# Retention gate of a hybrid decoder step by seven half-size products, its place in the retention loop given to a head's key and query projection, and two smaller reorderings

## The chip, the cores and the metric

One core of one Trainium2 chip runs the whole program. The metric is the time of one execution in microseconds on the device. A kernel's time is the median of several executions; one more execution is taken with the hardware profiler, and all rows below come from that one.

## What is computed

The reference is one layer of a decoder for 1024 prompt tokens and 8 sample tokens (1032 columns in all, model width 1024). The parts that matter here:

```python
hp = rmsnorm(xp, norm_mix)
qa, ka, va, qr, kr, vr, gr = split(hp @ w_in)        # widths 512 512 512 256 256 512 512
oa  = diff_attention(qa, ka, va)                     # 4 heads, two softmax maps each
s, o_r = retention(rotary(qr), rotary(kr) * 64**-.5, vr)   # 4 heads, 8 chunks of 128 tokens
r   = head_rms(o_r) * silu(gr)                       # the retention gate
xp  = xp + concat(head_rms(oa) * subln * (1 - lam_init), r) @ w_out
...                                                  # memory cross-attention
xp  = xp + square(relu(rmsnorm(xp) @ w_up)) @ w_down # hidden width 4096
```

All weights and activations are float32. A large product is made of three matmuls: both operands are split into a rounded high part and a low part, and high x high, high x low and low x high are summed.

## The kernel before

**Value blocks.** `token_block` computes a 1024 x 512 product over the model width 1024 with seven products of half the size in each direction instead of eight (a Strassen-like scheme, products numbered 1, 2, 6, 7, 4, 5, 3). Each product is 4 token tiles x 4 slices of 128 input rows x 3 terms = 48 matmuls of 256 columns; for the 8 sample rows four of the products add 8 narrow matmuls each (`psd`). The kernel runs it twice, for the attention values (`va`, PSUM tiles `vap_*`) and for the retention values (`vr`, tiles `vrp_*`). VectorE and ScalarE combine and scale the products and split the weights of the next one. `token_operands` loads four weight units per block through SyncE's DMA queue.

**Retention loop.** For each of 8 chunks of 128 tokens: four transposes of queries and keys (`tr`), scores (`sc`, masked on VectorE into `Sm`), the state update (`st`, added on VectorE into `S`), the output (`op`), then on ScalarE the squares of the output per head (`jk`, sums `s4`), on GpSimd their power -1/2 (`r4`), on VectorE the normalised output times the gate (`gate`, line 665), and in the next step four transposes of that (`trR`), a split into `rh` and `rl` (one buffer each), and two stores to DRAM through GpSimd's queue (`OPH`, `OPL`). Between these small matmuls TensorE does the gate projection of the same chunk, `grp`: 24 matmuls of 512 columns per chunk, dealt out 9 + 12 + 3 by `SEG`. After chunk 2 the gate of the sample rows follows (`decproj`, 16 matmuls, line 286 of the helper `dproj`). `decode_step`, in steps 0 to 3, does the sample rows' retention: GpSimd multiplies (`vb`, lines 703 and 714), VectorE state updates (`sn`). In the same steps ScalarE and VectorE rewrite half of the operand tiles `UH`, `UL` (`restore`).

**Attention.** `head_proj(0)` then makes the keys and queries of attention head 0 (144 matmuls of 344 columns, tiles `qkp`, results `kraw`, `qraw`) as filler that `fill(n)` deals out n matmuls at a time: 96 after the loop, 36 more (`START`) before the first score. `load_part` splits keys into `KA` and `KB` and copies each half to the other 64 partitions by DMA from GpSimd's queue; it splits queries into `Q`. Scores (`sp`) of map 0 and map 1 read `KA[0]`, `KB[0]` and `KA[1]`, `KB[1]`. VectorE forms `e` and its minimum `mn`, ScalarE the exponential; TensorE transposes the result (`trA`). The order of TensorE's instructions is the order of the program text (`pinned`); the other engines' order comes from the scheduler that respects `behind(...)` and `issue_after(...)`: an instruction stands behind a named one.

**Down projection.** Its left weights are loaded in four groups (`raw_d`, 8 transfers of 512 KB a group, `load_left`, line 2492), its hidden activations by `right_lower` (`raw_h`, two transfers of 516 KB per product, line 2375; products 1, 2, 6, 7, 4, 5, 3 again), all on SyncE's queue, which issues in order and waits at an instruction whose buffer is not free. TensorE works on `dn` tiles (line 2412), 169 matmuls in a stretch of 20 us.

Of the kernel before, what the change touches and what calls it, by code (L numbers as in the profile page):

```python
# [19 lines left out]
P = 128  # L20
# [28 lines left out]
def decoder_step(ctx: ExitStack, tc: tile.TileContext, i: dict, o: dict):  # L49
# [115 lines left out]
    ord_ = dram.tile([4, 8, P], F32, tag="ord", name="ord_")  # L165

# [17 lines left out]
    t_front, v_front = ExitStack(), ExitStack()  # L184
# [203 lines left out]
    with pool("a") as A:  # L388
# [6 lines left out]
        def decproj(units, name, PS, out, bufs=3):  # L395

            ps = PS.tile([P, 512], F32, tag="acc", name=name, bufs=bufs)

            dproj(ps, units)
            merge_parts(ps, out, name)  # L400
            return out

# [3 lines left out]

        def tokproj_parts(units, t, name, PS):
            ps = PS.tile([P, 512], F32, tag="acc", name=name, bufs=3)
            tk = slice(t * P, t * P + P)
            for kt in KT_PAIRS:  # L410
                w = [u[:, (kt // 4) * 512 : (kt // 4) * 512 + 512] for u in units[kt % 4]]
                mm(ps, UH[:, kt, tk], w[0], kt == 0, False)
                mm(ps, UH[:, kt, tk], w[1], False, False)
                mm(ps, UL[:, kt, tk], w[0], False, kt == 7)
                yield ps
# [64 lines left out]
        def token_block(ready, nm, out_dec, fetch, between, after):  # L480
# [12 lines left out]
            def scale(t):  # L493
                if t > 3 and nm == "vr":
                    return
                y = acc[t // 2][:, t % 2, :]
                cs = slice(256, 512) if t < 4 else slice(0, 512)
                nc.scalar.activation(y[:, cs], y[:, cs], AF.Copy, scale=rstd1[:, t : t + 1])

            order = (1, 2, 6, 7, 4, 5, 3)  # L500
            for n, q in enumerate(order):
# [13 lines left out]
                for pb in range(2):  # L515
# [14 lines left out]
                    with behind("Activation", "DVE"):  # L530
                        if q == 1:
                            nc.scalar.copy(lo[:, :, b], pv)
                        elif q == 2:
                            for j in range(2):
                                nc.scalar.activation(lo[:, j, a], pv[:, j, :], AF.Copy, scale=rstd1[:, 2 * pb + j : 2 * pb + j + 1])
# [7 lines left out]
                if q in (1, 2, 4, 5):  # L543
# [6 lines left out]
                    if q == 5:  # L550
                        merge_parts(psd, out_dec, nm)
                        nc.scalar.activation(out_dec, out_dec, AF.Copy, scale=rstd1[:8, 8:9])
# [35 lines left out]
        rot_va, rot_vr = {4: 8, 5: 0, 3: 1}, {1: 2, 2: 3, 6: 4, 7: 5, 4: 6, 5: 7}  # L588

        def after_va(q, acc):  # L590
# [8 lines left out]
            if q in rot_va:  # L599
                rotate(rot_va[q])  # L600

        def after_vr(q, acc):
            if q in rot_vr:
                rotate(rot_vr[q])
            if q == 5:
                nc.scalar.dma_start(vrd, vr8[:8])
                nc.scalar.activation(silu, half[:, 0:1], AF.Silu)
            if q in (5, 3):
                for u in range(2):
                    if q == 3:  # L610
# [2158 lines left out]
```

## Time and profile before

| | us |
|---|---|
| three runs | 1473.46, 1474.56, 1474.77 |
| median | 1474.56 |
| the profiled execution, its own time | 1475.19 |
| its span in the profile | 1473.4 |
| first matmul of the value blocks, first of the retention loop | 54.3, 143.4 |
| last `op` matmul of the loop, first score | 226.7, 249.6 |
| TensorE busy | 1455.7 |

The profiled execution took 0.63 us more than the median, and 1.8 us of it lie outside the span. Times of places in the program are microseconds from the start of the span. A busy TensorE is a sum of modelled matmul spans that overlap; what a stretch of matmuls really takes is read from the chain of work that ended last, where a run of matmuls stands with its start, its length and its count.

### The profile page before, as it was taken

The numbers are of one execution on the slowest core, as the hardware profiler recorded it, in microseconds if no ns is written. First come the engines' busy times: TensorE is split into PE (matmuls) and PEld (weight loads), VectorE is DVE, ScalarE is ACT, GpSimd is POOL, SyncE is SP. The second block draws the span as 40 slices with busy tenths as digits, with TensorE's granted clock in tenths as the row PEclk, the third lists the DMA queues.
The fourth block names the chain that finished last, engine by engine and source line by source line (L and its number), as shares of the span: only waits on it lengthen the run. The fifth ranks groups of instructions, "written<-read, shape, count | busy, mean of one in ns | idle before, by whom it ended". The sixth has DMA issues, their size and how long they took to land.

```text
span 1473.4 us, 28129 instructions
## 1 busy us (share of the span) xinstructions
PE 1455.7 (99%) x11013; PEld 1401.0 (95%) x11013; DVE 1107.9 (75%) x2263; ACT 679.7 (46%) x1327; POOL 314.4 (21%) x345
## 2 busy tenths in 40 slices
PE   9999999999999999999999999999999999999998
PEld 7899779999889999999999999999999999999998
DVE  7666536888867756567868988888888878787876
ACT  7434435666552441267436533343435443343454
POOL 0035433122304511224122000000002211110380
PEclk9999999999999999999999999999999999999998
DMA  8155738215957265654762444333446764536273
GB/s 295 62 188 171 205 70 192 72 34 159 283 169 269 100 209 170 177 178 122 236 234 77 151 159 158 138 136 133 149 159 216 262 213 144 173 105 200 71 130 116
DMA packets 129833, 238.98 MB, mean 162 GB/s; under 512 B 13606, under 2 KB 80987, under 8 KB 129572
## 3 DMA queue, kind: packets, MB, share of 16 engines
q1 hardware_dynamic: 91354, 170.66, 36.0%
q0 software_dynamic: 27472, 46.93, 11.8%
q10 hardware_dynamic: 10874, 19.60, 3.5%
q8 instruction: 86, 1.41, 0.4%
q14 instruction: 47, 0.39, 0.1%
HBM read 171.13 MB, written 58.92 MB: 156 GB/s over the span
## 4 chain that ended last, share of the span: by engine, by line
PE 88%; DVE 5%; DMA 2%; ACT 2%; issue 1%; POOL 0%; ACTq 0%; SPq 0%; DVEq 0%
PE dn L2412 20%; PE Z L2244 9%; PE qkp L75 6%; PE Y L2244 6%; PE X L2244 6%; PE mq L75 6%; PE pr_m L75 6%; PE pr_o L75 5%; PE grp L75 3%; PE sp L75 2%; PE mv L75 2%; PE mk L75 1%; PE av L75 1%; PE mpv L75 1%; PE vap_z L524 1%; PE vrp_z L524 1%
## 5 line engine op out<-in xcount | busy, mean ns | idle before, releaser
L2412 PE MATMUL dn<-UH,wd 128*128 128x258 f32 (+1 forms) x1800 | 326.6, 283 | 3.0 <-DVE c L2546 3.0
L2412 PEld LDWEIGHTS dn<-UH,wd 128*128 128x128 f32 x1800 | 279.6, 190 | 3.6 <-ACT wd L2388 2.6
L2412 PE MATMUL dn<-UL,wd 128*128 128x258 f32 x900 | 254.6, 283 | 0.0
L2412 PEld LDWEIGHTS dn<-UL,wd 128*128 128x128 f32 x900 | 170.5, 189 | 0.1
L2546 DVE TENSOR_TENSOR c<-c,dn 128x258 f32<-128x258 f32 (+1 forms) x217 | 89.1, 417 | 38.5 <-PE dn L2412 35.8
L2270 ACT ACTIVATE hq<-r 128x258 f32<-128x258 f32 x128 | 53.7, 421 | 117.4 <-DVE r L2269 117.3
L2244 PE MATMUL Z<-T_h,wu 128*128 128x258 f32 x512 | 98.1, 283 | 0.0
L2244 PE MATMUL X<-UH,wu 128*128 128x258 f32 x512 | 97.5, 282 | 0.0
L2388 ACT CAST wd<-raw_d 128x512 fp32r<-128x512 f32 x96 | 58.7, 619 | 82.0 <-PE dn L2412 77.3
L2052 ACT CAST wu<-raw_up 128x512 fp32r<-128x512 f32 x96 | 59.0, 616 | 61.0 <-PE Z L2244 52.6
L2381 ACT CAST UH<-raw_h 128x1032 fp32r<-128x1032 f32 x56 | 58.7, 1055 | 55.2 <-PE dn L2412 27.9
L2244 PEld LDWEIGHTS X<-UH,wu 128*128 128x128 f32 x512 | 81.3, 188 | 0.0
L2244 PEld LDWEIGHTS Z<-T_h,wu 128*128 128x128 f32 x512 | 81.3, 189 | 0.0
L2382 DVE TENSOR_TENSOR UL<-raw_h,UH 128x1032 fp32r<-128x1032 f32 x56 | 72.9, 1301 | 9.9 <-ACT UH L2381 9.9
L2389 DVE TENSOR_TENSOR wd<-raw_d,wd 128x512 fp32r<-128x512 f32 x96 | 72.3, 759 | 10.2 <-ACT wd L2388 10.2
L2281 POOL DMA_DIRECT2D HT<-ht x32 | 17.2, 536 | 292.1 <-DVE ht L2280 291.6
L2244 PE MATMUL Z<-T_l,wu 128*128 128x258 f32 x256 | 72.3, 282 | 0.0
L2244 PE MATMUL X<-UL,wu 128*128 128x258 f32 x256 | 72.3, 282 | 0.0
L129 ACT CAST wh_u<-raw_u 128x1024 fp32r<-128x1024 f32 x43 | 44.7, 1047 | 57.6 <-PE mq L75 39.9
L2053 DVE TENSOR_TENSOR wu<-raw_up,wu 128x512 fp32r<-128x512 f32 x96 | 64.8, 689 | 3.6 <-ACT wu L2052 3.6
L2402 POOL TENSOR_TENSOR raw_d<-raw_d,raw_d 128x512 f32<-128x512 f32 x16 | 22.1, 1384 | 197.0 <-DVE raw_d L2398 145.3
L130 DVE TENSOR_TENSOR wl_u<-raw_u,wh_u 128x1024 fp32r<-128x1024 f32 x39 | 48.6, 1257 | 20.2 <-ACT wh_u L129 20.0
(616 smaller groups left out, 4707.4 us busy)
## 6 DMA issues: line engine op xcount, KB each, us to landing
raw_u<-in_wall SPq DMA_DIRECT2D x49, 512.0 KB
HT<-ht POOLq DMA_DIRECT2D x32, 516.0 KB, 3.0
raw_h<-HT SPq DMA_DIRECT2D x32, 516.0 KB
raw_up<-in_wall SPq DMA_DIRECT2D x32, 512.0 KB
raw_d<-in_wall SPq DMA_DIRECT2D x32, 512.0 KB
HQ<-hq ACTq DMA_DIRECT2D x32, 387.0 KB
raw_h<-HQ SPq DMA_DIRECT2D x24, 516.0 KB
cmk<-in_cmk SPq DMA_DIRECT2D x16, 512.0 KB
```

Of the source, the lines that this page charges most:

```text
L75: pinned(nc.tensor.matmul(out, l, r, start=start, stop=stop))
L130: (lo_engine or nc.vector).tensor_sub(wl[:, :n], raw[:, :n], wh[:, :n].bitcast(F32))
L2052: nc.scalar.copy(w[:, :512], src)
L2053: nc.vector.tensor_sub(w[:, 512:], src, w[:, :512].bitcast(F32))
L2244: pinned(nc.tensor.matmul(ps, l, r[:, k, :], start=first and k == 0 and x == 0, stop=k == 3 and x == 2, skip_group_check=True))
L2270: nc.scalar.activation(h[:, PLACE[quad], :], r, AF.Square)
L2381: nc.scalar.copy(h, rv)
L2382: nc.vector.tensor_sub(l, rv, h.bitcast(F32))
L2388: nc.scalar.copy(w[:, :512], src)
L2389: nc.vector.tensor_sub(w[:, 512:], src, w[:, :512].bitcast(F32))
L2412: pinned(nc.tensor.matmul(ps[:, part], l, r[:, k, cq], start=first and k == 0 and x == 0, stop=k == 3 and x == 2, skip_group_check=True))
L2546: nc.vector.tensor_add(y, y, ps)
```

## The change

Four things are edited.

1. The gate becomes a third `token_block` (`ga`), between `va` and `vr`, with the sigmoid-weighted function applied where a value block scales. Its result goes to a DRAM tensor `gated` and is fetched again chunk by chunk (`fetch_gate`). `grp` and the sample rows' `decproj` go. The weights of the gate are laid out in DRAM as those of a value block. The rotations of queries and keys that ran beside `vr` now run beside `ga`.
2. In the retention loop `head_proj(0)` takes the place of `grp`: 8 filler matmuls ahead of the loop, 6 and 5 per step (`RFILL`), 96 in all; 36 are left between the loop and the first score. The transposes of the next chunk move ahead (`turn_step`); `brep` and `rb` are sent in the `vr` block; the weights of head 1 are split in steps 4 and 5.
3. `load_part` of heads 1 to 3 rounds and subtracts the keys of both maps in one instruction of 128 partitions each; the halves are then placed by four DMAs of GpSimd's queue and two of SyncE's. For head 0 the four-instruction form stays, in two pieces of 344 columns. `load_values(0)` and the loads of heads 2 and 3 move by one step.
4. `load_left` of the second group stands behind the last `raw_h` load of the first.

```diff
-        rot_va, rot_vr = {4: 8, 5: 0, 3: 1}, {1: 2, 2: 3, 6: 4, 7: 5, 4: 6, 5: 7}
+        rot_va, rot_ga = {4: 8, 5: 0, 3: 1}, {1: 2, 2: 3, 6: 4, 7: 5, 4: 6, 5: 7}
...
+        def after_ga(q, acc):
+            if q in rot_ga:
+                rotate(rot_ga[q])
+            for t in {5: range(4), 3: range(4, 8)}.get(q, ()):
+                nc.scalar.dma_start(gated[t * P : t * P + P, :], acc[t // 2][:, t % 2, :])
...
-        token_block(op_va, "va", vdec[:8], rot_va, after_va, op_vr)
+        op_ga, op_vr = token_operands(U_TOK + 8, "ga"), token_operands(U_TOK + 4, "vr")
+        token_block(op_va, "va", vdec[:8], rot_va, after_va, op_ga)
+        ga8 = A.tile([P, 512], F32, tag="t1", name="ga_8", bufs=1)
+        token_block(op_ga, "ga", ga8[:8], rot_ga, after_ga, op_vr, AF.Silu)
...
-            grp = tokproj_parts(units, t, f"grp_{t}", PS)
-            for _ in range(SEG[0]):
-                next(grp)
...
+        filler = head_proj(0)
+        dec = decode_step(0)
+        next(dec)
+        gate = fetch_gate(0)
+        turned = turn_step(0)
+        fill(RFILL[0])
+        for t in range(8):
+            qb, kT = turned
...
+            if t < 7:
+                turned = turn_step(t + 1)
+            if scaled:
+                with behind("DVE"):
+                    next(scaled)
+            fill(RFILL[1])
...
+            if pend:
+                pend()
+            fill(RFILL[2])
...
         def load_part(h, cs):
...
+            if h:
+                nc.scalar.copy(KA[1][:, cs], kraw[:, cs])
+                for x in (lo, hi):
+                    nc.gpsimd.dma_start(KA[0][x, cs], KA[1][lo, cs])
+                nc.vector.tensor_sub(KB[1][:, cs], kraw[:, cs], KA[1][:, cs].bitcast(F32))
...
+                if h:
+                    K1 = (KA, KB)[m][1]
+                    nc.sync.dma_start(K1[lo, cs].bitcast(F32), K1[hi, cs].bitcast(F32))
...
-        fill(36)
+        load_stacks(0)
+        for c in range(2):
+            for _ in load_part(0, slice(c * CH, c * CH + CH)):
+                pass
+        filler = chain(filler, rest())
+        fill(28)
         to_operand(gate, P, 7, "7", ("ah", "al", 2))
-        until(0, 1, 0)
+        fill(6)
+        to_operand(lasts[0], 8, 8, "d", ("ah", "al", 2))
...
-            load_left((0, 1) if g == 0 else range(4))
+            with tc.issue_after(seen["SP"]) if g == 1 else nullcontext():
+                load_left((0, 1) if g == 0 else range(4))
...
-START = 36
+START = 2
...
-SEG = (3, 4, 0)
+RFILL = (8, 6, 5)
```

What that does to the order is seen at three places.

SyncE's queue in the down projection, before. `raw_h0_3_0` is the first half of the hidden activations of product 3 in group 0; `raw_d1_...` are left weights of group 1; `c12` and `c21` are residual rows.

```order
L2375 DMA raw_h0_5_0_14176<-HT_75 128x4x258
L2375 DMA raw_h0_5_2_14180<-HT_75 128x4x258
L2492 DMA raw_d1_0_0_14436<-in_wall 128x1024
L2492 DMA raw_d1_1_0_14438<-in_wall 128x1024
L2375 DMA raw_h0_3_0_14184<-HQ_74 128x4x258
L2492 DMA raw_d1_2_0_14440<-in_wall 128x1024
L2375 DMA raw_h0_3_2_14188<-HQ_74 128x4x258
L2361 DMA c12_13489<-X3_73 128x516 x4
```

The same place of the changed kernel:

```order
L2392 DMA raw_h0_5_0_14375<-HT_75 128x4x258
L2392 DMA raw_h0_5_2_14379<-HT_75 128x4x258
L2392 DMA raw_h0_3_0_14383<-HQ_74 128x4x258
L2392 DMA raw_h0_3_2_14387<-HQ_74 128x4x258
L2378 DMA c12_13688<-X3_73 128x516 x4
L2509 DMA raw_d1_0_0_14635<-in_wall 128x1024
L2509 DMA raw_d1_0_1_14636<-in_wall 128x1024
L2509 DMA raw_d1_1_0_14637<-in_wall 128x1024
```

Three loads of the second group no longer stand between the loads of the first group's products 5 and 3.

TensorE in chunk 7 of the retention loop, before: the scores, the state, the transposed gate of chunk 6, and the first seven of twelve gate matmuls.

```order
L75 MATMUL sc_2267<-qblk_1566,kT_2255 128x256 x2
L75 MATMUL st_2272<-vr_1210,qk_491 64x128 x4
L78 MATMUL trR_2277<-ident,gate_2214 128x128 x4
L75 MATMUL grp_2257<-wh_u_1492,UH 128x512
L75 MATMUL grp_2257<-wl_u_1493,UH 128x512
L75 MATMUL grp_2257<-wh_u_1492,UL 128x512
L75 MATMUL grp_2257<-wh_u_1600,UH 128x512
```

The same place of the changed kernel, with all that stands between `st` and the first `op` matmul:

```order
L75 MATMUL sc_2584<-qblk_2028,kT_2526 128x256 x2
L75 MATMUL st_2589<-vr_1696,qk_492 64x128 x4
L75 MATMUL qkp_0_1_2482<-UL,wh_u_1954 128x344
L75 MATMUL qkp_0_1_2482<-UH,wl_u_1955 128x344
L75 MATMUL qkp_0_1_2482<-UH,wh_u_1954 128x344
L75 MATMUL qkp_0_1_2482<-UL,wh_u_1954 128x344
L75 MATMUL qkp_0_1_2482<-UH,wl_u_1955 128x344
L75 MATMUL qkp_0_1_2482<-UH,wh_u_1954 128x344
L75 MATMUL op_2604<-vr_1696,Sm_2587 128x128
```

Twelve matmuls of 512 columns (and in the chunks before the transposes of the next chunk) give way to six of 344, and `trR` moves behind `op`.

GpSimd from the last chunk's factor `r4_7` to the first key copies of head 0, before (`rh_7` and `rl_7` are the split gate of the last chunk, `VL_0` the low part of the values):

```order
L141 TENSOR_TENSOR r4_7_2330<-s4_7_2329,half_64 128x4
L678 DMA OPL_71<-rl_d_2352 128x4x8
L1051 MEMSET ah_0_0_0_2703 128x128
L678 DMA OPH_70<-rh_7_2427 128x4x128
L678 DMA OPL_71<-rl_7_2428 128x4x128
L1051 MEMSET al_0_0_0_2704 128x128
L995 TENSOR_TENSOR VL_0_2748<-vraw_0_2572,VH_0_2747 128x512 x2
L968 DMA KA0_0_2513<-KA0_0_2513 64x688
L970 DMA KB0_0_2515<-KB0_0_2515 64x688
```

And in the changed kernel:

```order
L141 TENSOR_TENSOR r4_7_2634<-s4_7_2633,half_64 128x4
L984 DMA KA0_0_2675<-KA0_0_2675 64x344
L986 DMA KB0_0_2677<-KB0_0_2677 64x344
L984 DMA KA1_0_2676<-KA1_0_2676 64x344
L986 DMA KB1_0_2678<-KB1_0_2678 64x344
```

The key copies of head 0 now follow the last factor directly, where two stores and the values' low part stood between.

## Rows read from the trace of the kernel before

**Rows 1.** The page: busy us, share and instructions of each engine.

```profile
PE 1455.7 (99%) x11013; PEld 1401.0 (95%) x11013; DVE 1107.9 (75%) x2263; ACT 679.7 (46%) x1327; POOL 314.4 (21%) x345
```

**Rows 2.** TensorE's waits, by what ended them: us in total, times, longest.

```profile
PE dn L2412 <- DVE c L2546: 3.0, 2, 2.4
PE trA L78 <- DVE e L1034: 2.1, 2, 1.4
PE sp L75 <- DVE mn L1019: 1.8, 2, 1.0
```

**Rows 3.** The chain in the block va: start, us, what, count.

```profile
54.29 5.68 PE vap_x L524 x48
59.98 0.94 PE vap_d L547 x8
```

**Rows 4.** The chain in the retention loop and behind it.

```profile
173.12 3.71 PE grp L286 x16
...
187.10 2.10 PE grp L75 x9
...
191.40 2.80 PE grp L75 x12
...
230.90 1.13 DVE gate L665 x4
...
234.68 9.44 PE qkp L75 x60
...
244.66 2.27 DVE wl_u L130 x2
```

**Rows 5.** Windows: length, busy us (count) PE, PEld, DVE, ACT, POOL; PEclk, DMA, GB/s.

```profile
99.00:106.00 7.00, 6.83 (x58) 6.42 (x56) 5.51 (x8) 4.21 (x7) 2.61 (x3) 1.00 0.70 231
...
156.00:166.00 10.00, 10.00 (x62) 8.12 (x61) 4.76 (x13) 3.65 (x13) 4.54 (x5) 1.00 1.04 362
187.10:197.12 10.02, 10.02 (x61) 8.10 (x61) 3.52 (x10) 3.03 (x13) 5.03 (x5) 1.00 0.43 105
...
1160.00:1180.00 20.00, 20.00 (x169) 20.00 (x169) 17.90 (x29) 9.06 (x15) 1.67 (x1) 1.00 0.81 260
1180.00:1200.00 20.00, 17.62 (x134) 17.45 (x134) 13.54 (x24) 9.60 (x13) 0.00 (x0) 0.91 0.82 281
```

**Rows 6.** Issue of `raw_h0_3_0`, and the first copy of it: start, us, what.

```profile
1174.51 0.38 SPq L2375 DMA_DIRECT2D raw_h<-HQ  x1
...
1182.78 1.06 ACT L2381 CAST UH<-raw_h 128x1032 fp32r<-128x1032 f32 x1 [5.95 <-DMA raw_h<-HQ]
```

**Rows 7.** The chain in the same place.

```profile
1163.76 3.88 DMA raw_h<-HT
...
1177.60 7.84 DMA raw_h<-HQ
...
1188.26 11.80 PE dn L2412 x84
```

**Rows 8.** GpSimd in step 1 of the retention loop: start, us, what.

```profile
164.93 1.03 POOL L141 TENSOR_TENSOR r<-s,half 128x4 f32<-128x4 f32 x1 [4.35 <-DVE s L140]
...
166.53 1.91 POOL L714 TENSOR_TENSOR vb<-sn,qkd 128x1024 f32<-128x1024 f32 x1
169.05 0.80 POOL L678 DMA_DIRECT2D OPH<-rh  x1 [0.61 <-ACT rh L675]
```

**Rows 9.** Key copies (line 968) to landing; VectorE's split of one map's keys.

```profile
DMA to landing us min/median/max: 2.3/4.4/7.7
...
276.80 0.86 DVE L969 TENSOR_TENSOR KB<-kraw,KA 64x688 fp32r<-64x688 f32 x1
```

**Rows 10.** TensorE idle at the first scores of head 0, in brackets.

```profile
262.42 0.41 PE L75 MATMUL sp<-KA,Q 128*128 128x320 f32 x1 [0.85 <-DVE mn L1019]
```

**Rows 11.** Stores of the loop, 145 to 165, then 165 to 200: KB, us to landing.

```profile
OPH<-rh POOLq DMA_DIRECT2D x1, 256.0 KB, 9.3
...
OPH<-rh POOLq DMA_DIRECT2D x3, 256.0 KB, 2.9
```

More of the change, by code (lines that the diff above doesn't have):

```diff
@@ L478, in decoder_step, with token_block @@
         PS = f_ps.enter_context(pool("f_ps", space=PSUM))
-        def token_block(ready, nm, out_dec, fetch, between, after):
+        def token_block(ready, nm, out_dec, fetch, between, after, func=AF.Copy):
             acc = []
@@ L629, in decoder_step, with fill, until @@
+        def fill(n):
+            for _ in range(n):
+                next(filler, None)
+        def until(*key):
+            while key not in done:
+                next(filler)
         pin[0] = True
-        op_vr = token_operands(U_TOK + 4, "vr")
-        token_block(op_va, "va", vdec[:8], rot_va, after_va, op_vr)
+        op_ga, op_vr = token_operands(U_TOK + 8, "ga"), token_operands(U_TOK + 4, "vr")
+        token_block(op_va, "va", vdec[:8], rot_va, after_va, op_ga)
+        ga8 = A.tile([P, 512], F32, tag="t1", name="ga_8", bufs=1)
@@ L730, in decoder_step, with fetch_gate @@
             nc.vector.tensor_copy(kT, tr[:, 256:512])
-            if t == 6:
-                with behind("DVE"):
-                    next(scaled)
-            grp = tokproj_parts(units, t, f"grp_{t}", PS)
-            for _ in range(SEG[0]):
-                next(grp)
+            return qb, kT
+        def fetch_gate(t):
+            if t < 7:
+                gate = A.tile([P, 512], F32, tag="gate", name=f"gate_{t}", bufs=3)
+            else:
+                last = G.tile([P, T], F32, tag="raw", name="gate_7", bufs=3)
+                gate = last[:, :512]
+                lasts.append(last[:8, 512:1024])
+            nc.sync.dma_start(gate, gated[t * P : t * P + P, :])
+            return gate
+        S, pend, scaled, lasts = None, None, None, []
+        filler = head_proj(0)
+        pin[0] = True
+        dec = decode_step(0)
[5 more added lines that the diff above has]
+            qb, kT = turned
             sc = PS.tile([P, 512], F32, tag="sc", name=f"sc_{t}", bufs=1)
@@ L1265, in decoder_step @@
         items = [(h, pr, kg) for h in range(4) for pr in range(4) for kg in range(pr + 1)]
-        done = set()
         EARLY, LATE = slice(0, 2 * CH), slice(2 * CH, NT)
@@ L1271, in rest @@
                 yield from head_proj(h)
-        filler = head_proj(0)
         decode = decode_steps()
-        def fill(n):
-            for _ in range(n):
-                next(filler, None)
-        def until(*key):
-            while key not in done:
-                next(filler)
-        pin[0] = True
-        fill(36)
-        to_operand(gate, P, 7, "7", ("ah", "al", 2))
-        until(0, 1, 0)
-        with behind("Activation", "DVE"):
-            head_units(1)
-        load_stacks(0)
-        for _ in load_part(0, EARLY):
-            pass
-        filler = chain(filler, rest())
+        pin[0] = True
+        load_stacks(0)
+        for c in range(2):
+            for _ in load_part(0, slice(c * CH, c * CH + CH)):
+                pass
+        with behind("Activation"):
+            nc.scalar.activation(A.tile([P, 1], F32, tag="pre", name="pre"), half[:, 0:1], AF.Exp)
+        filler = chain(filler, rest())
+        fill(28)
+        to_operand(gate, P, 7, "7", ("ah", "al", 2))
+        fill(6)
+        to_operand(lasts[0], 8, 8, "d", ("ah", "al", 2))
         par = operand_steps()
```

228 lines of the change are left out of this document (104 added, 124 removed).

## The prediction

> **What bounds the kernel now.** I read the busy shares first: TensorE is busy 1455.7 us of a span of 1473.4 [rows 1]; the next engine, VectorE, is at 75%. So the time is TensorE's work plus the few places where it waits. The list of its waits says how little that is: the largest are 3.0 us for the combination `c` of the down projection, 2.1 us for `e` ahead of the transposes of attention and 1.8 us for `mn` ahead of the scores [rows 2]. An edit can therefore gain in two ways: fewer or shorter matmuls, or one of these waits. It can lose in one: by taking away filler behind which the other engines now finish unseen. The third view, the chain of waits in the retention loop, shows an unbroken row of TensorE pieces [rows 4]: every wait in this loop is covered today. The windows add how much the other engines do there [rows 5].
>
> **The change part by part.** All sums are against the profiled execution, 1475.19 us, which lies 0.63 us over the median of 1474.56.
>
> *1. Products.* Nine `grp` matmuls take 2.10 us and twelve 2.80 us, so 0.2325 us each [rows 4]. The loop has 8 x 24 = 192 of them, 44.64 us; the sample rows' 16 take 3.71 us [rows 4]. Removed: 48.35 us. Added is a block of the form of `va` and `vr`, for which `va` has the price: 48 matmuls in 5.68 us, 0.1183 us each, and 8 narrow ones in 0.94 us [rows 3]. Seven products make 7 x 48 = 336 matmuls, 39.76 us, and four groups of narrow ones 3.76 us: 43.52 us. Net **-4.8 us**. This is the surest term, as both prices are of the same operations on the same operand types. Its check is arithmetic: seven eighths of 44.64 us would be 39.06, so half-width matmuls cost 0.7 us more for the same columns.
>
> The rows put a 256-column matmul at 0.1183 us and a 512-column one at 0.2325 us, nearly the ratio of the columns [rows 3, 4]. The Trainium skill, "TensorE: Matmul & The Clock Gate", section "Back-to-back issue gap", speaks against such a halving: in a stream of weight loads and matmuls it gives about 81 ns for 128 columns and 131 ns for 512, so a matmul four times as wide costs only 1.6 times as much. Interpolated (an estimate from that page of the Trainium skill), 256 columns would cost some 98 ns, and term 1 would be 336 x 0.098 + 3.8 - 208 x 0.131 = 9.5 us lost. Both rows here contradict that, and the measurement decides.
>
> *2. Boundaries between forms of matmul.* A step of the loop has two groups of filler instead of three between the small matmuls. No row prices a boundary; nine matmuls in a row cost no more apiece than twelve [rows 4], so it is between nothing and about half a matmul, 0.1 us: 0 to -0.8 us for eight steps. I take **-0.4**.
>
> *3. The second group's left weights.* In the window 1160 to 1180 TensorE does 169 matmuls, in 1180 to 1200 only 134 [rows 5]. The missing 35 at 0.118 us are 4.1 us: 2.4 us idle [rows 2, 5], and the rest slower matmuls, since the granted clock, at 1.00 (2.4 GHz) before, is 0.91 in the mean of this window, so at the lower level for part of it [rows 5], and 84 `dn` matmuls take 11.80 us, 0.140 each [rows 7]. The cause can be read: `raw_h0_3_0` is issued at 1174.51, behind two weight loads, and its first copy starts at 1182.78, with ScalarE 5.95 us idle for it [rows 6]; the second half takes 7.84 us [rows 7]. The same kind of load shortly before takes 3.88 us [rows 7]. With the weights behind it, it should land some 3.5 to 4.4 us earlier, which covers the 2.4 us and so the clock's fall. Its own buffer does not come free earlier, so the issue time stays; what goes is the traffic beside it. **-4.1** (0 to -4.1). The price could be that group 1 is late. Its first weights are put off by the two halves of `raw_h0_3` and the residual rows alone, some 4 us, and product 3 lies between, whose 84 matmuls in the chain are 11.8 us [rows 7]; I take nothing for it, and would lose the same 4 us if that cover were gone.
>
> *4. The retention loop with less cover.* A step lasts 10.02 us [rows 5]. Without its 5.58 us of `grp` and with 11 matmuls of `head_proj` at 9.44/60 = 0.157 us [rows 4] it lasts 4.44 + 1.73 = 6.2 us. The other engines must fit in that. VectorE is busy 4.76 us in a step of the first half and 3.52 later [rows 5]; added are about 0.5 us of `kraw`/`qraw`, so 5.3: it fits, with order and latency against it. In steps 4 and 5 come weight splits of 2.27/2 = 1.14 us each [rows 4]. GpSimd in step 1 has `r` 1.03, two `vb` of 1.91, and three stores of about 0.8: 7.2 us [rows 8], over 6.2 by about one. So some steps wait a few tenths and step 1 nearly a microsecond: **+1.9** (0 to +5, the upper end being 0.6 us in each of eight steps). At zero it would be hidden by the move of `trR` behind `op`, which gives the gate's chain almost a whole step.
>
> *5. From the loop to the first score.* Today the last gate is ready at 232.03 [rows 4], 5.3 us behind the last `op`, and the first score comes at 249.6. Afterwards the five fills of the last step and 36 more, 41 x 0.157 = 6.4 us, and some 1.5 us of transposes cover this stretch: 7.9 us. The keys of head 0 need that gate chain on VectorE (5.3), a split (about 0.5 for half the columns, half of the 0.86 of [rows 9], and as much again behind it), the issue on GpSimd (0.55), and the landing, 2.3 to 7.7 us, median 4.4 [rows 9]: 8.7 us at the lowest landing, 10.7 at the median. The wait is then 0.8 to 2.8, with a slow landing about 5; I take **+1.7**, nearer the middle, as little else is on the DMA queues there. Against it stands the 0.85 us that TensorE idles at 262.42 for `mn` [rows 10]: four splits of the next head's weights at 1.14 us [rows 4], which made VectorE late, are then done in the loop: **-0.85** (0 to -0.85).
>
> *6. One more block.* The change from `va` to `vr` costs 0.17 us in its window (7.00 less 6.83 [rows 5]); one more such place, with the sigmoid's function loaded there: **+0.3** (0.17 to 1).
>
> *7. Attention.* For three heads one split on 128 partitions takes the place of two on 64 (0.86 us each [rows 9]): VectorE saves some 3 x 1.4 = 4 us with the pieces. The waits for `e` and `mn`, 3.9 us less the 0.85 above [rows 2, 10], bound the gain at 3; two copies more by DMA per key could be late, +1. I take **-1.0** (+1 to -2.6).
>
> Sum: -4.8 - 0.4 - 4.1 + 1.9 + 1.7 - 0.85 + 0.3 - 1.0 = -7.25, so 1467.9 for such a profiled execution and 1467.3 by the median; I say 1467.5. All good ends: about -12 (1462.7); all bad ones of terms 2 to 7: +7.
>
> **The rivals.** *Loop and prelude at their upper ends* (terms 4 and 5 at +4 and +4.5 instead of +1.9 and +1.7): about 1472.5. For it: the loop has no filler left to spare, and three engines are within a microsecond of its length [rows 5, 8]. Against: `jk`'s and the gate's chain now have a step to finish.
>
> *The down projection's wait stays.* If `raw_h0_3_0` is slow for other reasons than the two weight loads (the residual rows `c12` in the same queue, or the window's traffic of 260 GB/s as such [rows 5]), term 3 is 0: 1471.4. For it: a DMA share of 0.81 before the wait begins; against: 3.88 us for the same load ahead of it [rows 7].
>
> *Slower: the stores of the loop hold up `rh` and `rl`.* These have one buffer each, so the next split waits until the store has landed. `OPH` took 9.3 us in the stretch 145 to 165, where the DMA share is 1.04, and 2.9 us in the later one [rows 5, 11]. In 10 us steps this was hidden; in steps of 6.2 us it decides from a landing of about 4.5 us on (a step less the split and the issue). Three early steps at 9.3 would cost 3 x 4.8 = 14 us, in place of the loop's 1.9: 1467.5 + 12 = 1479.5. Against: the vr block's loads, which fill the queues early in the loop, are the same in number, but the gate weights' loads now lie ahead of it.
>
> *Weight loads bind the half-width matmuls.* The mean busy time of a weight load is 1401.0/11013 = 0.127 us [rows 1], over the 0.1183 of a 256-column matmul; if each new matmul were held to that, 336 + 32 of them would take 46.7 us, term 1 would shrink to -1.6, and the time be 1470.7. `va` has the same loads at 0.1183 already [rows 3], which speaks against it. The section of the Trainium skill, "TensorE: Matmul & The Clock Gate", "Back-to-back issue gap", lets both operations set the spacing; by its figures the time would be 1481.8.
>
> *The change doesn't do what it says* (as many matmuls as before, since one product is recomputed): the order of the instructions excludes it.
>
> **How the numbers follow.** Forecast, 1464.5 to 1470.5: 0.63. Upper ends in loop and prelude, 1470.5 to 1474: 0.14. The wait in the down projection stays, 1471.4: 0.12. Slower by the stores, 1478 to 1485: 0.08. Weight loads, 1470.7: 0.02. Better than 1464.5: 0.01. About 0.2%, 2.95 us, is what a measurement of this kernel can tell from no change, so faster ends at 1471.6 and slower begins at 1477.5. Faster gets the forecast, half of the second case, half of the third and the small ones: 0.63 + 0.07 + 0.06 + 0.03 = 0.79; slower the stores: 0.08; same the rest: 0.13. The range runs from 1463, all good ends, to 1474.
>
> **What would show it.** Right: `ga` as seven products of 5.7 us in the chain; loop steps of 6.2 to 6.7 us, with VectorE or GpSimd in the chain for tenths; a wait of 1 to 3 us for the key copies before the first score; 1180 to 1200 with about 169 matmuls and a granted clock of 1.00. Wrong: steps of 8 us and more, with `rh` or `rl` idle for `OPH` or `OPL`; `ga` matmuls at more than 0.12 us; ScalarE still 4 us idle for `raw_h` at product 3, or `dn` waiting at the start of group 1; a first score more than 14 us behind the last `op`.

## The result: 0.2% slower, where 0.5% faster was forecast

| | before | changed |
|---|---|---|
| median, us (20 runs each) | 1473.66 | 1476.71 |
| lowest and highest | 1472.09, 1475.72 | 1473.67, 1480.42 |
| the profiled execution, us | 1475.19 | 1476.23 |
| ratio | | 1.0022, 95% interval 1.0016 to 1.0029 |

The changed kernel loses about 3 us; 7 less had been forecast, and the range ended at 1474.0. The page of the changed kernel answers [rows 1]: TensorE is as full as it was, with 160 more matmuls in 1.3 us less busy time.

```profile
PE 1454.4 (99%) x11173; PEld 1408.3 (96%) x11173; DVE 1118.1 (76%) x2278; ACT 680.4 (46%) x1335; POOL 318.1 (22%) x349
```

Its waits answer [rows 2]. The one in the down projection is nearly gone, as forecast, though not through the edit, as will be seen; those of attention have grown, by count above all. The wait for `mn` of [rows 10], which term 5 of the prediction counted as won, is still there: 0.91 us at 258.69.

```profile
PE trA L78 <- DVE e L1053: 3.6, 5, 1.3
PE sp L75 <- DVE mn L1038: 2.4, 4, 1.0
PE dn L2429 <- DVE c L2564: 1.2, 3, 0.6
...
PE ct L75 <- ACT sq L1096: 0.8, 1, 0.8
```

```profile
258.69 0.42 PE L75 MATMUL sp<-KA,Q 128*128 128x320 f32 x1 [0.91 <-DVE mn L1038]
```

The chain in the new block and in one step of the loop (start, us, what, count) answers [rows 3, 4]. The gate's products cost what `va`'s did, 43.6 us from 99.43 to 143.06, and a step of the loop takes 6.28 us, from 199.92 to 206.21 here; nothing but TensorE stands in it.

```profile
99.43 5.68 PE gap_x L507 x48
105.11 0.94 PE gap_d L530 x8
...
137.36 5.71 PE gap_y L507 x48
```

```profile
199.92 0.86 PE sc L75 x4
200.79 0.59 PE st L75 x8
201.38 0.59 PE tr L78 x4
201.96 0.95 PE qkp L75 x6
...
202.93 2.05 PE op L75 x16
204.99 0.44 PE trR L78 x4
205.42 0.79 PE qkp L75 x5
206.21 0.86 PE sc L75 x4
```

**Where the lead is.** The first score of head 0 on TensorE and the first `e` on VectorE that reads it, in the kernel before and in the changed one (start, us, what):

```profile
249.59 0.28 PE L75 MATMUL sp<-KA,Q 128*128 128x256 f32 x1
...
250.34 0.28 DVE L1019 CUSTOM_DVE_ANT_0 e<-sp,M 128x128 f32<-128x128 f32 x1
```

```profile
244.34 0.28 PE L75 MATMUL sp<-KA,Q 128*128 128x256 f32 x1
...
248.12 0.28 DVE L1038 CUSTOM_DVE_ANT_0 e<-sp,M 128x128 f32<-128x128 f32 x1
```

TensorE is 5.25 us earlier, VectorE only 2.2: its lag has grown from 0.75 to 3.8 us. From the last `gate` to this `e` VectorE is busy but for 0.4 us; the eight splits of head 0's keys and queries are 4.2 us of that. The `gate` itself had waited for its factor from GpSimd, which issued two stores of the loop just before making it:

```profile
240.19 1.13 DVE L704 SCALAR_TENSOR_TENSOR gate<-op,r,gate 128x128 f32<-128x128 f32 x4 [1.18 <-POOL r L141]
```

From the first score on the order of TensorE's instructions is the same in both kernels, matmul for matmul, so the same matmul can be looked up in both traces and its times subtracted. The difference is -5.3 us at the first score, -3.9 at 254, -1.7 at 273, +0.6 at 323, +1.8 at 333, +3.7 at 397: **attention gives back 9 us.** It stays near +4 until the down projection, where it falls from +4.4 to +0.2 (from the kernel before losing time, as will be seen), and ends at +0.9.

The places where the lead goes are TensorE's idle times in front of these instructions (in brackets, with what ended them), and two stretches in which the granted clock is under 1.00. The rows are the changed kernel's.

```profile
271.20 0.55 PE L78 MATMUL trA<-ident,e 128*128 128x128 f32 x3 [0.83 <-DVE e L1053]
...
314.00 0.55 PE L78 MATMUL trA<-ident,e 128*128 128x128 f32 x3 [0.33 <-DVE e L1053]
...
323.32 0.83 PE L75 MATMUL ct<-ones,sq 128*128 128x1 f32 x6 [0.82 <-ACT sq L1096]
...
392.68 0.42 PE L75 MATMUL sp<-KA,Q 128*128 128x320 f32 x1 [0.97 <-DVE mn L1038]
...
399.73 0.55 PE L78 MATMUL trA<-ident,e 128*128 128x128 f32 x3 [1.28 <-DVE e L1053]
```

Windows of the changed kernel (columns as in [rows 5]):

```profile
318.00:334.00 16.00, 15.18 (x98) 14.55 (x97) 10.40 (x25) 7.85 (x15) 4.10 (x7) 0.89 0.43 100
388.00:402.00 14.00, 11.31 (x88) 8.93 (x90) 11.31 (x34) 8.11 (x22) 1.61 (x3) 0.88 1.22 359
```

In the first window of the kernel before the clock is 1.00 and 113 matmuls are done instead of 98:

```profile
318.00:334.00 16.00, 15.75 (x113) 15.22 (x113) 12.04 (x28) 9.90 (x19) 5.21 (x8) 1.00 0.39 89
```

A mean of 0.89 over 16 us and one of 0.88 over 14 us are some 1.7 us of work each: two falls to the lower level (1.2 GHz) cost 3.4 us. The first, from 325, comes behind the waits at 314 and 323. The second, from 393 to 397, comes behind the wait at 392.68 and ahead of the one at 399.73.

### The profile page after: what moved, and what is told of

Same layout as the page of the kernel before. It is cut to its first block, busy times and chain, and to the rows that moved or that the text cites. A ratio compares the mean times of both kernels' runs of the same rounds, so it can differ in the third digit from the quotient of the medians.

```text
span 1474.5 us, 28598 instructions
## 1 busy us (share of the span) xinstructions
PE 1454.4 (99%) x11173; PEld 1408.3 (96%) x11173; DVE 1118.1 (76%) x2278; ACT 680.4 (46%) x1335; POOL 318.1 (22%) x349
## 4 chain that ended last, share of the span: by engine, by line
PE 84%; DVE 7%; DMA 3%; issue 2%; ACT 2%; POOL 1%; SPq 0%; DVEq 0%; ACTq 0%; POOLq 0%
PE dn L2429 20%; PE Z L2261 9%; PE qkp L75 6%; PE Y L2261 6%; PE X L2261 6%; PE mq L75 6%; PE pr_m L75 6%; PE pr_o L75 2%; PE mv L75 2%; PE mk L75 1%; PE sp L75 1%; PE mpv L75 1%; PE av L75 1%; PE vap_z L507 1%; PE gap_z L507 1%
## 5 line engine op out<-in xcount | busy, mean ns | idle before, releaser
L75 PE MATMUL qkp<-UH,wh_u 128*128 128x344 f32 x192 | 63.6, 331 | 0.3 <-DVE gate L704 0.3
```

Of the source, the lines that this page charges most:

```text
L75: pinned(nc.tensor.matmul(out, l, r, start=start, stop=stop))
```

## Experiments

Each run is compared with runs of the kernel before on the same chip, by the ratio with its 95% interval; 0.001 is 1.5 us. Profiles are single executions, so a profile shows where time goes, the ratio how much.

**The changed kernel again.**

> The changed kernel again, to have it on the same chip as the next three. In the profile TensorE reaches the first score 5.4 us earlier than before and has lost 9.5 us by 397 us. Every theory: 1.5 to 4.5 us slower than before here.

Run e1: 1475.85 us, ratio 1.0019 (1.0011 to 1.0028). The loss stands on another chip.

**Theory A: pairs of weight splits.** VectorE makes the low parts of the weights of heads 2 and 3 (1.22 us each) in pairs in the changed kernel, with one `e` between the two, around the waits at 271 and 314. The pair at 271:

```profile
268.99 1.23 DVE L130 TENSOR_TENSOR wl_u<-raw_u,wh_u 128x1024 fp32r<-128x1024 f32 x1
...
271.06 1.22 DVE L130 TENSOR_TENSOR wl_u<-raw_u,wh_u 128x1024 fp32r<-128x1024 f32 x1
```

```diff
-                if x == 1 and h < 2:
-                    with tc.issue_after(seen["ACT"]):
-                        head_units(h + 2)
+                if x == 0 and h < 2:
+                    head_units(h + 2)
```

> The changed kernel with the loads of the weights of heads 2 and 3 back at the first step of a head, as before. Theory A (VectorE has no room in heads 0 and 1, and the pairs of weight splits at 269 to 272 and 311.8 to 315, back to back between the score steps, make it late): their waits and the clock's fall at 325 go, 2 to 4 us faster than the changed kernel. Theory B (the new placing of the keys of heads 1 to 3 makes scores or transposes late): within 1 us of the changed kernel.

Run e2: 1475.63 us, ratio 1.0014 (1.0005 to 1.0022): 0.7 us under the changed kernel, inside the uncertainty. In its profile the two waits and the fall of the clock are gone, but TensorE waits 1.35 us at 251 and 2.8 at 396. Moving the splits moves the waits. (This profile is the fastest of the run's executions, 2.6 us under its median.)

**Theory B: the new placing of keys, undone.**

```diff
-            if h:
+            if False:
                 nc.scalar.copy(KA[1][:, cs], kraw[:, cs])
...
-            for m in range(0 if h else 2):
+            for m in range(2):
...
-                if h:
+                if False:
                     K1 = (KA, KB)[m][1]
```

> The changed kernel with the keys of heads 1 to 3 split map by map and copied as before. Theory A (VectorE binds in attention): 1 to 3 us slower than the changed kernel, since VectorE gets some 4 us of splits back. Theory B (the new placing is late): 3 to 6 us faster than it.

Run e3: 1476.92 us, ratio 1.0028 (1.0019 to 1.0037). No gain, so the placing alone isn't what costs; the sign is theory A's, the size (1.3 us) not clear of the noise.

**The second group's left weights, undone.**

```diff
-            with tc.issue_after(seen["SP"]) if g == 1 else nullcontext():
-                load_left((0, 1) if g == 0 else range(4))
+            load_left((0, 1) if g == 0 else range(4))
```

> The changed kernel with the second group's left weights at their old place in the queue. By the two traces the stretch of the down projection gained 3.4 to 3.9 us; every theory on attention: 3 to 4.5 us slower than the changed kernel. If the wait there had gone for another reason: within 1 us of it.

Run e4: 1475.90 us, ratio 1.0020 (1.0008 to 1.0031): the same as the changed kernel. With the old order in the queue there is no wait either; its windows, to be read against [rows 5]:

```profile
1160.00:1180.00 20.00, 20.00 (x169) 20.00 (x169) 19.12 (x29) 11.67 (x18) 3.47 (x2) 1.00 0.65 212
1180.00:1200.00 20.00, 20.00 (x169) 20.00 (x169) 14.87 (x26) 9.12 (x13) 0.00 (x0) 1.00 0.89 300
```

That points away from the weights as the cause of the wait of 2.4 us.

**The kernel before, profiled once more.**

> The kernel before, profiled once more. Theory C (the wait of 2.4 us for product 3 in the down projection belongs to the one profiled execution, not to the kernel): no wait over 1 us in 1160 to 1200, granted clock 1.00 there, about 1472 us. If the wait belongs to the kernel: 134 or so matmuls in that window again, and 1474 to 1476 us.

Run e5: 1472.29 us. The stretch has no wait and a full clock:

```profile
1160.00:1180.00 20.00, 20.00 (x170) 20.00 (x169) 19.21 (x30) 9.66 (x15) 2.30 (x2) 1.00 0.76 250
1180.00:1200.00 20.00, 20.00 (x169) 19.99 (x168) 14.47 (x24) 10.54 (x14) 0.00 (x0) 1.00 0.91 309
```

The same matmul stands 2.6 us earlier in it from 1192 on than in the first profile. The wait belonged to that one execution.

**Only the fourth edit, on the kernel before** (the `-` lines of the diff above, put in).

> The kernel before with the fourth edit alone, the second group's left weights behind the first group's last hidden activations. Theory C (the wait in the down projection belonged to one execution): within 1 us of before. By the prediction's third term: 4 us faster.

Run e12: 1473.49 us, ratio 1.0002 (0.9989 to 1.0014). The edit is worth nothing, in either kernel.

**VectorE's lag at the first score.**

```diff
-RFILL = (8, 6, 5)
+RFILL = (8, 5, 4)
...
         pin[0] = True
+        fill(16)
         load_stacks(0)
```

> The changed kernel with 16 of the 96 filler matmuls moved from the loop to behind it (8 ahead, 5 and 4 per step, 16 more behind). Theory A (VectorE reaches the first score late, and TensorE's lead is lost to it): steps of 5.9 us, the lag of the first `e` behind the first score falls from 4.2 to about 2 us, 1 to 2.5 us faster than the changed kernel. If the loss comes from the attention's own order: within 1 us of it. If the loop has no room: slower by up to 2.5 us.

Run e6: 1475.65 us, ratio 1.0014 (1.0004 to 1.0025). The first score comes at 244.62 and the first `e` at 247.59: the lag falls from 3.8 to 3.0 us, less than expected, though the score is only 0.3 us later, so the loop had this room. At 323 the profile is 1.5 us ahead of the second profile of before (e1: 1.0 us behind). But all of it is lost at 396, in one wait of 3.0 us:

```profile
396.55 0.55 PE L78 MATMUL trA<-ident,e 128*128 128x128 f32 x3 [3.01 <-DVE e L1053]
```

Half right; what it showed is a second limit.

**Two cures that failed on the way.** The values of head 0 at their old step, since GpSimd's split of them runs beside an `e` of 1.65 us:

```diff
-                if x == 0 and h:
+                if x == 0:
                     load_values(h)
...
-            if g == -1:
-                with tc.issue_after(seen["ACT"]):
-                    load_values(0)
```

> The changed kernel with the values of head 0 split at the first step of head 0. Theory D (GpSimd's split of the values at 258.4 runs beside the `e` of 1.65 us, usual 0.75, and makes VectorE late): the long `e` goes, 0.5 to 1.5 us faster than the changed kernel. Theory A: within 1 us of it.

Run e7: 1478.17 us, ratio 1.0037 (1.0023 to 1.0050): slower, with a wait of 2.4 us for `mn` at 261.5. The keys of head 0 in one piece:

```diff
-        for c in range(2):
-            for _ in load_part(0, slice(c * CH, c * CH + CH)):
-                pass
+        for _ in load_part(0, EARLY):
+            pass
```

> The changed kernel with the first two thirds of head 0's keys and queries split in one piece of 688 columns instead of two of 344: four splits of 0.87 instead of eight of 0.52 on VectorE, four key copies fewer on GpSimd. Theory A (VectorE's queue ahead of the first `e`): 0.5 to 1 us faster. If the landing of the key copies bounds the first scores: slower by up to 1 us, since each copy is later and longer.

Run e8: 1476.33 us, ratio 1.0024 (1.0012 to 1.0036): no gain.

**Theory E: SyncE's queue.** Where the lead ends, at 396, VectorE stands idle for a transfer, `x_half`, and TensorE for VectorE. In SyncE's queue of the changed kernel two key copies of head 3 now stand ahead of it, and the row above them waits for its own transfer:

```profile
383.53 0.32 SPq L1129 DMA_DIRECT2D rbh<-hrow  x1
...
384.97 0.47 SPq L995 DMA_DIRECT2D KA<-KA  x1
385.54 0.54 SPq L995 DMA_DIRECT2D KB<-KB  x1
387.11 2.89 SPq L918 DMA_DIRECT2D ck<-in_cache_kT  x4
390.10 1.72 SPq L1353 DMA_DIRECT2D x_half<-in_xT  x3
...
398.50 0.52 DVE L1367 TENSOR_TENSOR x_half<-pr_half,x_half 128x344 f32<-128x344 f32 x1 [2.38 <-DMA x_half<-in_xT]
```

Before (second profile), the issue was at 386.30:

```profile
386.30 1.51 SPq L1342 DMA_DIRECT2D x_half<-in_xT  x3
...
393.92 0.51 DVE L1356 TENSOR_TENSOR x_half<-pr_half,x_half 128x344 f32<-128x344 f32 x1
```

```profile
396.22 0.55 PE L78 MATMUL trA<-ident,e 128*128 128x128 f32 x3 [1.41 <-DVE e L1034]
```

The last row is TensorE's wait at this place in the kernel before. In the changed kernel's own profile it is no longer than that, 1.28 us at 399.73: the fall of the clock from 393 has made TensorE late first. Where no fall comes ahead of it, in e2 and e6, it is 2.8 and 3.0.

The key placing of the third edit alone on the kernel before (the code of the `load_part` diff ahead of the prediction; the weight units and the values of head 0 stay at their old steps):

> The kernel before with the third edit alone: keys of heads 1 to 3 split on 128 partitions, two copies per part in SyncE's queue. By the prediction's seventh term 1 us faster. Theory E: VectorE is relieved early in attention and held up by `x_half` late, 0.5 to 3 us slower than before. If the queue costs nothing where there is no lead: within 0.5 us.

Run e16: 1477.06 us, ratio **1.0024 (1.0015 to 1.0034)**: about 3.5 us slower, as much as the whole change. `x_half` is issued at 391.56 and VectorE is idle 1.66 us for it, but TensorE's wait behind it is shorter than before. Its profile also has two falls of the clock, at 392, ahead of that wait, and at 426, of 1.7 us each:

```profile
398.03 0.55 PE L78 MATMUL trA<-ident,e 128*128 128x128 f32 x3 [0.90 <-DVE e L1047]
```

```profile
388.00:402.00 14.00, 12.07 (x102) 9.73 (x101) 12.22 (x39) 7.06 (x20) 1.61 (x3) 0.88 1.14 366
420.00:434.00 14.00, 13.49 (x91) 13.05 (x89) 9.26 (x18) 6.31 (x11) 1.93 (x3) 0.88 0.53 184
```

That this placing costs time is shown; that it does so through `x_half` is not shown by this run.

Three tries to mend it by moving work. The key copies in GpSimd's queue:

```diff
-                    nc.sync.dma_start(K1[lo, cs].bitcast(F32), K1[hi, cs].bitcast(F32))
+                    nc.gpsimd.dma_start(K1[lo, cs], K1[hi, cs])
```

> The changed kernel with the two further key copies of each part in GpSimd's queue instead of SyncE's. Theory E (these copies wait in SyncE's queue, `x_half` behind them is issued some 5 us later than before, and VectorE stands 2.3 us idle for it at 396): `x_half` is issued 2 to 4 us earlier, that idle time falls under 1 us, 1 to 2 us faster than the changed kernel. If the issue is late because of `hrow` and `rbh` alone: within 1 us of it.

Run e9: 1478.38 us, ratio 1.0033 (1.0023 to 1.0043). `x_half` is issued at 388.34 and no longer waited for, as theory E said; but the copies stand behind each other on GpSimd, and TensorE waits 1.47 us for `KB` at 384, and 1.6 us for VectorE at 428. The weight units two steps apart:

```diff
-                if x == 1 and h < 2:
+                if x in (2, 6) and h < 2:
                     with tc.issue_after(seen["ACT"]):
-                        head_units(h + 2)
+                        head_unit(h + 2, (x - 2) // 4)
```

> The changed kernel with the two weight units of heads 2 and 3 prepared at the steps 2 and 6 of a head instead of both at step 1. Theory A (two splits back to back make VectorE late for the transposes at 271 and 314): the waits of 0.8 and 0.3 us there and the fall of the clock at 325 go, 2 to 3.5 us less by 332 us in the profile, 1 to 3 us faster than the changed kernel in the median. If the pairs don't matter: within 1 us of it.

Run e10: 1477.62 us, ratio 1.0025 (1.0014 to 1.0035). The waits at 271 and 314 are gone and the profile is 1.6 us ahead at 330, but 0.95 and 1.48 us are lost at 346 and 352 and 2.5 at 399. All three edits together (16 fillers, key copies on GpSimd, units two steps apart):

> Three edits on the changed kernel together: 16 fillers behind the loop, the weight units at steps 2 and 6, the further key copies in GpSimd's queue. If A and E name the places where the lead of 5.4 us was lost: 3 to 5 us faster than the changed kernel, so 0 to 2.5 us faster than the one before. If VectorE's load as a whole binds attention and a wait avoided comes back at the next step: within 1.5 us of the changed kernel.

Run e11: 1479.30 us, ratio 1.0035 (1.0024 to 1.0047): 3.4 us ahead at 329, behind by 5 at 398. By the ratio the slowest but one: cures by moving work don't add up.

`x_half` through GpSimd's queue:

```diff
             for n in range(3):
-                fetch_x(n)
+                xc, ft, cs = piece(n)
+                nc.gpsimd.dma_start(xc, i["xT"][:, ft, cs])
```

> The changed kernel with the first three loads of `x_half` in GpSimd's queue, past SyncE's, and the key copies where they are. Theory E (SyncE's queue is held by the key copies): VectorE's idle time of 2.3 us for `x_half` goes and 1 to 2 us are won. Theory F: the wait goes and less than 1 us is won, as others take its place.

Run e14: 1477.31 us, ratio 1.0029 (1.0017 to 1.0041). No cure: GpSimd issues it at 389.8 to 392.0, and it takes 10.4 us to land. VectorE waits 2.5 us.

**VectorE's work taken away instead of moved.**

```diff
         nc.scalar.copy(wh[:, :n], raw[:, :n])
+        if not low:
+            return wh, wh
...
-                uqk.setdefault(h, []).append(unit(U_QK + 2 * h + x))
+                uqk.setdefault(h, []).append(unit(U_QK + 2 * h + x, low=h < 2))
```

> The changed kernel without the four weight splits of heads 2 and 3 on VectorE (four times 1.22 us); the high part of these weights stands in for the low part, so the keys and queries of the two heads lose precision and nothing else changes. Theory A (those splits, standing back to back, cost TensorE its lead in heads 0 and 1): some 4 us less at 332 us in the profile, no fall of the clock at 325. Theory F (attention has a second limit behind the first, SyncE's late `x_half` at 396 above all): most of it is lost again at 396, the median 0 to 1.5 us under the changed kernel. If A alone holds: 3 to 5 us under it.

Run e13: 1472.52 us, ratio **0.9987 (0.9978 to 0.9997)**. (The high part counts twice in these heads, so more than precision is lost there; the instructions differ by the four splits alone.) Four splits are 4.9 us of VectorE; against the changed kernel at 1.0019 to 1.0022 the time falls by 0.0032 to 0.0035, which is 4.7 to 5.2 us. **VectorE binds in heads 0 and 1**, with the waits and the fall of the clock that follow from it: its profile has no fall between 240 and 440. That the two amounts agree is in part chance, since the time holds the fall's 1.7 us. The same splits were not taken out of the kernel before, so the run tells what binds and not by itself what the change made worse. And the wall at 396 stands in its profile, 3.0 us:

```profile
396.06 0.55 PE L78 MATMUL trA<-ident,e 128*128 128x128 f32 x3 [3.02 <-DVE e L1055]
```

This matmul starts at 396.22, 396.27, 396.55 and 396.06 in the second profile of before, the units at step 0, the 16 fillers and this run, though the last three were 1.5 to 2 us ahead of the first at 387. With the 16 fillers and `x_half` through GpSimd as well:

> Both of these with 16 fillers behind the loop (low part of the weights of heads 2 and 3 left out as before). Theory A and E together (splits and queue are all that costs the lead): 6 to 9 us faster than the changed kernel, so 3 to 6 faster than before. Theory F with still further limits: 2 to 4 us faster than the changed kernel.

Run e15: 1471.74 us, ratio 0.9988 (0.9979 to 0.9997): no more than the splits alone. VectorE still waits 2.0 us for `x_half`. The forecast of both theories added, 3 to 6 us under the kernel before, failed: this cure of `x_half` is none.

**The key copies out of the way.** Head 3's keys in the old form, with the 16 fillers:

```diff
-            if h:
+            if h in (1, 2):
                 nc.scalar.copy(KA[1][:, cs], kraw[:, cs])
...
-            for m in range(0 if h else 2):
+            for m in range(0 if h in (1, 2) else 2):
...
-                if h:
+                if h in (1, 2):
                     K1 = (KA, KB)[m][1]
```

> The changed kernel with 16 fillers behind the loop (as in the run of that edit alone) and head 3's keys in the old form, so that no key copy stands ahead of x_half in SyncE's queue. Theory E (those copies make x_half late): its issue comes 1 to 3 us earlier relative to TensorE, the wait of 3.0 us at 396 falls under 1.5, 1 to 3 us faster than the changed kernel. Theory G (the transfers of 382 to 400 fill the DMA engines, and x_half takes 8 to 10 us to land wherever it stands): within 1 us of the run without this edit, so 0 to 1 us under the changed kernel.

Run e17: 1474.55 us, ratio 1.0001 (0.9990 to 1.0012). `x_half` isn't waited for any more, and the wait of 3.0 us is 1.41, as in the kernel before:

```profile
398.47 0.55 PE L78 MATMUL trA<-ident,e 128*128 128x128 f32 x3 [1.41 <-DVE e L1053]
```

Against the second profile of before, `x_half` is issued 2.2 us later and TensorE is 2.0 us later, where in e6 the issue was 0.8 us later and TensorE 1.9 us ahead. So theory E holds for the wait, and theory G (the DMA engines are full wherever it stands) is not needed for it: an earlier issue in SyncE's queue is enough. By the ratio the loss against before is gone, but the interval overlaps that of e6, so the gain of this edit by itself is not shown.

**Gate and loop without the third edit** (all keys old, weight units at step 0, 16 fillers; the values of head 0 stay at their new step):

> The first two edits and the fourth, without the third: all keys split and copied as before, the weights of heads 2 and 3 at the first step of a head as before, 16 fillers behind the loop. If the gate and the loop gain 5 us and the third edit is what loses them: 1472 or under, 1 to 3 us faster than before. If attention gives back TensorE's lead whatever the third edit does: within 2 us of before, or slower.

Run e18: 1472.55 us, ratio **0.9993 (0.9981 to 1.0004)**. Some 4 us better than the changed kernel, and by its middle 1 us better than before, which the interval doesn't tell from nothing. By the number that is the second expectation: without the two parts of the third edit the change is not slower any more, but attention still gives back nearly all of the lead. `x_half` is issued at 384.23 and TensorE's wait at 395 is 0.9 us:

```profile
395.28 0.55 PE L78 MATMUL trA<-ident,e 128*128 128x128 f32 x3 [0.90 <-DVE e L1053]
```

Of the 4.6 us lead that its profile has at the first score (against the second profile of before), 2.0 are gone by 262 (waits for VectorE), and 1.6 go between 386 and 395, where a fall of the clock costs 1.7; 0.9 is left at 396.

## Why the prediction was wrong

*Products (term 1, -4.8).* Right. 43.6 us for the block, 43.5 forecast. Of the rivals, the weight loads that bind half-width matmuls are out: 48 of them take 5.68 us in `ga` as in `va`.

*Boundaries, loop, prelude (terms 2, 4, 5, 6; sum +3.5, with the 0.85 that goes at 262 counted with attention).* Too dark up to the first score. Steps of 6.0 to 6.3 us (7.0 in the one with the sample rows' output), where 6.2 plus waits of 1.9 were given, with TensorE waiting 0.5 us in all between the loop's start and the first score; and no wait of 1.7 for the key copies, which landed in 2.1 to 2.2 us where 4.4 had been taken. With term 1, a lead of 1.3 us was forecast at the first score, and 5.25 came. The rival of the loop's stores holding up `rh` and `rl` did not reach TensorE: `OPH` landed in 2.9 us in the loop (median), under the 4.5 us from which it would have decided. The 0.85 us of term 5 was not won at all (0.91 us at 258.69), though the weight splits that it blamed had gone into the loop.

*The prelude's cover (term 5) is the first step that failed, though not in its number:* it asked only whether TensorE would wait for the first keys. It didn't; but VectorE, which in the kernel before had 23 us between the last `op` and the first score to clear its queue and now has 8, reaches the first `e` 3.8 us behind the score, and the wait comes as many small ones later. "Who is late next" was asked of one instruction and not of the engine's queue.

*Attention (term 7, -1.0, and the 0.85).* The step that decided. -1.85 was forecast, +9 came in the profiles. The waits for `e` and `mn` of [rows 2] were read as what could be won; they were the sign that VectorE had no room, so a TensorE that comes earlier waits there. In the kernel before VectorE is busy 18.72 of 20 us where head 0 begins:

```profile
260.00:280.00 20.00, 19.15 (x125) 18.34 (x124) 18.72 (x52) 12.21 (x25) 1.90 (x5) 1.00 0.17 44
```

The third edit was priced by the VectorE time that it saves; the two copies in SyncE's queue got +1 as a possible lateness of their keys, when they also delay what stands behind them: `x_half`, issued 4.6 us behind the second of them. The placing alone on the kernel before costs 3.5 us (e16; its profile has 3.4 us of work lost by falls of the clock), and taking it off head 3 takes the late `x_half` away (e17). The moved weight units of heads 2 and 3 have no term in the sum; they came in pairs onto a VectorE that is the bound (e13).

Where each run loses its lead is seen when the start of the same matmul in the second profile of before is subtracted, at the first score, at 266, 388 and 399 of that profile (us, minus is ahead):

| | first score | 266 | 388 | 399 |
|---|---|---|---|---|
| changed kernel | -5.7 | -3.6 | +1.3 | +3.5 |
| e2, weight units at their old step | -5.7 | -2.0 | -1.8 | +0.1 |
| e3, keys in the old form | -4.5 | -2.4 | +1.1 | +2.6 |
| e13, four splits left out | -5.0 | -2.9 | -2.8 | -0.2 |
| e18, both old, 16 fillers | -4.6 | -2.5 | -2.5 | -0.9 |

Between 266 and 388 the lead goes where the units stand at the new step (4.9 and 3.5 us) and stays where they don't, or where their splits are left out (0.2 us lost at most); ahead of 266 and at 388 to 399 every run loses some. The profiles of e2 and e3 are the fastest executions of their runs, so the table tells where and not how much. By the ratios putting back one part of the third edit is not enough: with the keys put back the ratio is 1.0028 (e3), with the units put back 1.0014 (e2), with both and 16 fillers 0.9993 (e18). Both put back without the fillers was not run.

*The down projection (term 3, -4.1).* Failed at its evidence. The mechanism was read from the rows of one execution, and the wait isn't in the second profile of before (e5), nor in that of the changed kernel with the old order (e4). Its median had already been 0.6 us under its profile; the wait's 4 us fit in the spread of the runs (1472.1 to 1475.7). The edit alone has a ratio of 1.0002 (e12), no gain. This was 4.1 of the 7.25 us forecast.

*The range* ended at 1474 on the slow side, since the one slower rival was put in the loop. That attention could give back all that TensorE gained wasn't among the rivals.

What stays open: why the falls of the clock come in one profile and not in another of nearly the same idle times (e3 has the fall at 393 without the wait for `x_half`; e2 and e13 wait 2.8 and 3.0 us at 396 without a fall); what in the key placing costs e16 its 3.5 us; and how the 9 us of the profiles split exactly between splits, queue and clock, since the cures don't add.

## What to carry to other kernels

When a change frees the engine that is 99% busy, look at the engine next to it over the whole stretch behind the gain, not at the one instruction that joins them: if it is at 90% there, the lead is only as long as that engine's own, and work moved onto that stretch has a price even where it was only moved by one step. Every DMA put into an in-order queue is priced by what stands behind it, to the next instruction that someone waits for, however far down the program. And a wait that stands in one profile is a fact about one execution: before it carries half of a forecast, it should be in the profile of a second one.

## What the runs showed of the hardware

A VectorE instruction took up to twice its time and more beside a GpSimd one that had not started later: `e` of 512 columns 1.65 us in the changed kernel, usually 0.75, while GpSimd split the values.

```profile
258.37 2.99 POOL L1014 TENSOR_TENSOR VL<-vraw,VH 128x512 fp32r<-128x512 f32 x2 [4.20 <-ACT VH L1012]
...
258.56 1.65 DVE L1053 SCALAR_TENSOR_TENSOR e<-e,mn,e 128x512 f32<-128x512 f32 x1
```

In e7, where the split stands at 255.3, the same `e` took 0.74:

```profile
260.31 0.74 DVE L1053 SCALAR_TENSOR_TENSOR e<-e,mn,e 128x512 f32<-128x512 f32 x1
```

It is so in the kernel before too: the `e` beside the split took 1.32 us at 348.68 and 1.81 at 394.10. Where `e` started first, at 302.44 in the changed kernel, it took 0.75, and the first half of the split beside it 1.50 us instead of 1.29.

A fall of TensorE's clock to its lower level, behind idle times of 0.3 to 3 us, cost about 1.7 us in most profiles (windows of 0.88 and 0.89). In two, of e14 and e17, the one at 323 to 325 cost twice that; e17's window:

```profile
320.00:334.00 14.00, 13.18 (x75) 12.80 (x74) 7.31 (x16) 5.22 (x9) 3.05 (x6) 0.76 0.48 113
```
